# Head pairs of a delta-rule recurrence: one at a time in three interleaved generators, or two at a time in two

## The chip, the cores and the metric

The kernel runs on one core of one Trainium2 chip. The metric is device time in microseconds (us) for one execution of the whole program; before the change it is 2546.13 us, the median of three runs (2545.74 to 2553.71).

## What is computed

A decoder trunk of two residual layers, sequence 256, width 2048, all in fp32. The even layer (block attention and gated mixing) and the two gated MLPs are not touched. The odd layer is RWKV-7 time mixing with 32 heads of 64:

```python
def rwkv7_time_mix(h, mu, w_rkv, w_o, ...):
    r = xr @ w_rkv[0]; k = xk @ w_rkv[1]; v = xv @ w_rkv[2]
    w_log = -jax.nn.softplus(-(w0 + jnp.tanh(xw @ w1) @ w2)) - 0.5
    decay = jnp.exp(-jnp.exp(w_log))
    a = jax.nn.sigmoid(a0 + (xa @ a1) @ a2)
    g = jax.nn.sigmoid(xg @ g1) @ g2
    kk = k * k_k / max(norm of k * k_k per head, 1e-12)
    k = k * (1.0 + (a - 1.0) * k_a)
    def step(state, inp):                       # 256 steps in order
        sa = jnp.einsum('bhvk,bhk->bhv', state, -kk_t)
        state = state * w_t + sa[..., None] * (kk_t * a_t) + v_t[..., None] * k_t
        return state, jnp.einsum('bhvk,bhk->bhv', state, r_t)
    o = group norm of the outputs over each head, plus bonus sum(r * k * r_k) * v
    return (o * g) @ w_o
```

## The kernel before

**Dense products** are made exact by splitting fp32 operands into a high and a low part of type fp32r: ScalarE casts `w_hi` (L99, L115), VectorE subtracts `w_lo` (L101, L118). A K tile of a product with 256 positions is one matmul of 512 columns (`w_hi` by high and low input, L138 or L141) and one of 256 (L139).

**The odd layer's main loop** (`rwkv`, L679 to L685) goes over 16 pairs of heads, 128 channels each. The sequence is cut into 4 chunks of 64 positions, so that the recurrence becomes small matrix products in plain fp32. Three generators work on three pairs at a time, and `weave` merges their steps by weights: `pair_in(i)` makes k, r, the decays `E`, `Ei` and the norms `n4` and `bo` of pair i (32 dense K tiles); `pair_solve(i-1)` builds `bk` and the products `AQ`, and inverts the triangular matrices by 4 doubling levels of two products each (L840 into `Y`, L848 into `X`) and a last pair (L860, L868); `pair_out(i-2)` runs the 4 chunks one after the other (L904 and L906, ScalarE copy to `R`, L913, VectorE copy to `UV`, L918 and L932), then group norm and the gate product. A fp32 matmul stands as two records in the trace.

Two more iterations (i = 16, 17) drain the pipeline. Beside them `early` does the part of the output projection whose inputs are ready: `KO` = 12 of its 16 K tiles, for all 16 blocks of output. What is left (4 K tiles, `w_o1b`) is done after the loop by `residual`, two output blocks at a time: their sum is added into `x` (L191), and ScalarE, VectorE (L255) and GpSimd make the input of the next norm.

**Order.** The `weave` order is only a priority: a scheduler sets each engine's static order at build time, and engines then run in order, waiting by semaphores. `feed` casts the dense weights ahead of `dense_f` by `AHEAD` = 5 pieces. PSUM has 8 banks under 5 names (`BANKS`): `pd` dense, `pa` and `sc` two each, `po` and `pi` one each.

## Time and profile before

| | us |
|---|---|
| median of three runs | 2546.13 |
| the profiled execution | 2545.33 |
| its span on the core | 2543.5 |
| of it, from the first `pair_in` to the last `early` matmul (1223.6 to 1764.9) | 541.3 |
| of it, `residual` after that (1764.9 to 1797.5) | 32.6 |

PE is TensorE, PEld its weight loads, DVE VectorE, ACT ScalarE, POOL GpSimd. A PE that is busy need not be at its peak: ends of matmuls are modelled, and a small product keeps the engine from the next one longer than it streams. The distance from the start of one group of matmuls to the start of the next is therefore the better measure, and the timeline views give it.

### The profile page before, as it was taken

How to read it: one execution, taken by the hardware profiler on the slowest of the kernel's cores; microseconds unless marked ns; L12 is line 12 of the kernel's file. 1: busy time of each engine (PE TensorE's matmuls, PEld its weight loads, DVE VectorE, ACT ScalarE, POOL GpSimd, SP SyncE). 2: the span in 40 equal slices, each digit the busy share in tenths (PEclk: the TensorE clock that was granted, in tenths of full speed). 3: DMA queues.
4: the chain of work that ended last, by engine and by line, in shares of the span. 5: the costliest groups of instructions: out<-in, count | busy, mean ns of one | idle time of the engine just before them, and what ended most of it. 6: DMA issues, size and time to landing. Idle time of an engine off the chain costs nothing.

```text
span 2543.5 us, 49471 instructions
## 1 busy us (share of the span) xinstructions
PE 2497.4 (98%) x18884; PEld 2120.0 (83%) x18884; DVE 1871.7 (74%) x3813; ACT 1290.8 (51%) x2754; POOL 489.0 (19%) x810
## 2 busy tenths in 40 slices
PE   8999999999999999989999999999999999999998
PEld 6888888888888888878777777778888888888887
DVE  7768778888888645578777777877888888885444
ACT  6568655555555444454444444535555555554443
POOL 3100122222222100000233333321322222220000
PEclk9999999999999999999999999999999999999999
DMA  7554555555555666646322322235555555556664
GB/s 262 181 175 158 165 181 187 193 186 191 190 188 190 189 185 189 186 144 185 118 81 87 95 88 78 81 109 170 172 191 188 191 189 190 190 182 194 187 190 144
DMA packets 126493, 422.30 MB, mean 166 GB/s; under 512 B 14129, under 2 KB 20657, under 8 KB 126257
## 3 DMA queue, kind: packets, MB, share of 16 engines
q1 hardware_dynamic: 126112, 418.82, 52.6%
q8 instruction: 148, 2.42, 0.4%
q14 instruction: 89, 0.72, 0.1%
q10 hardware_dynamic: 144, 0.33, 0.0%
HBM read 417.00 MB, written 2.10 MB: 165 GB/s over the span
## 4 chain that ended last, share of the span: by engine, by line
PE 90%; DVE 5%; ACT 2%; POOL 1%; issue 1%; DMA 1%; SPq 0%; POOLq 0%; DVEq 0%; ACTq 0%
PE pd L170 20%; PE pd L171 11%; PE pi L170 10%; PE po L170 10%; PE pi L171 6%; PE po L171 6%; PE pd L138 5%; PE pd L139 3%; PE pd L173 1%; PE sc L614 1%; DVE w_lo L101 1%; PE po L906 1%; PE sc L913 1%; PE pd L215 1%; PE pd L214 1%
## 5 line engine op out<-in xcount | busy, mean ns | idle before, releaser
L101 DVE TENSOR_TENSOR w_lo<-w_raw,w_hi 128x512 fp32r<-128x512 f32 (+1 forms) x1392 | 1054.9, 788 | 317.4 <-ACT w_hi L99 292.2
L99 ACT CAST w_hi<-w_raw 128x512 fp32r<-128x512 f32 (+1 forms) x1392 | 792.3, 614 | 502.9 <-PE pd L170 139.8
L170 PE MATMUL pd<-xc,w_hi 128*128 128x512 f32 x1500 | 528.1, 392 | 1.6 <-DVE xc L255 1.0
L171 PE MATMUL pd<-xc,w_lo 128*128 128x256 f32 x1600 | 433.8, 281 | 0.0
L170 PEld LDWEIGHTS pd<-xc,w_hi 128*128 128x128 f32 x1500 | 281.4, 188 | 60.6 <-issue 2.7
L171 PEld LDWEIGHTS pd<-xc,w_lo 128*128 128x128 f32 x1600 | 301.9, 189 | 8.4
L170 PE MATMUL po<-xc,w_hi 128*128 128x512 f32 x750 | 264.8, 393 | 0.0
L170 PE MATMUL pi<-xc,w_hi 128*128 128x512 f32 x750 | 263.4, 392 | 0.0
L171 PE MATMUL po<-xc,w_lo 128*128 128x256 f32 x800 | 217.3, 282 | 1.9 <-DVE w_lo L101 1.9
L171 PE MATMUL pi<-xc,w_lo 128*128 128x256 f32 x800 | 216.9, 281 | 0.0
L170 PE MATMUL pd<-hc,w_hi 128*128 128x512 f32 x602 | 211.4, 393 | 0.0
L171 PE MATMUL pd<-hc,w_lo 128*128 128x256 f32 x616 | 169.7, 279 | 0.0
L170 PEld LDWEIGHTS po<-xc,w_hi 128*128 128x128 f32 x750 | 140.7, 188 | 29.5 <-issue 1.5
L170 PEld LDWEIGHTS pi<-xc,w_hi 128*128 128x128 f32 x750 | 140.7, 188 | 28.5
L138 PE MATMUL pd<-mx,w_hi 128*128 128x512 f32 x416 | 163.2, 418 | 0.0
L118 DVE TENSOR_TENSOR w_lo<-w_raw,w_hi 128x256 fp32r<-128x256 f32 x352 | 150.0, 461 | 16.7 <-ACT w_hi L115 15.6
L171 PEld LDWEIGHTS po<-xc,w_lo 128*128 128x128 f32 x800 | 150.9, 189 | 6.9 <-DVE w_lo L101 2.7
L243 POOL TENSOR_TENSOR sqacc<-sqacc,sq 128x256 f32<-128x256 f32 x70 | 61.8, 883 | 491.1 <-ACT sq L235 470.5
L171 PEld LDWEIGHTS pi<-xc,w_lo 128*128 128x128 f32 x800 | 150.9, 189 | 4.3
L115 ACT CAST w_hi<-w_raw 128x512 fp32r<-128x512 f32 x176 | 107.0, 620 | 79.2 <-PE pa L695 34.4
L170 PEld LDWEIGHTS pd<-hc,w_hi 128*128 128x128 f32 x602 | 112.8, 187 | 26.4
L139 PE MATMUL pd<-mx,w_lo 128*128 128x256 f32 x448 | 128.4, 298 | 0.0
(328 smaller groups left out, 4665.4 us busy)
## 6 DMA issues: line engine op xcount, KB each, us to landing
w_raw<-w_up SPq DMA_DIRECT2D x352, 512.0 KB, 4.1
w_raw<-w_dn SPq DMA_DIRECT2D x160, 512.0 KB, 3.7
w_raw<-w_kr SPq DMA_DIRECT2D x64, 512.0 KB, 4.3
w_raw<-w_eva SPq DMA_DIRECT2D x48, 512.0 KB, 4.2
w_raw<-w_out SPq DMA_DIRECT2D x32, 512.0 KB, 4.5
w_raw<-w_v SPq DMA_DIRECT2D x32, 512.0 KB, 3.8
w_raw<-w_evb SPq DMA_DIRECT2D x31, 512.0 KB, 4.4
w_raw<-w_dn SPq DMA_DIRECT2D x32, 256.0 KB, 2.7
```

Of the source, the lines that this page charges most:

```text
L99: nc.scalar.copy(hi[h], raw[h])
L101: nc.vector.tensor_sub(lo[h], raw[h], hi[h])
L115: nc.scalar.copy(hi[:, j:j + 512], raw[:, j:j + 512])
L118: nc.vector.tensor_sub(lo[:, j:j + pieces], raw[:, j:j + pieces], hi[:, j:j + pieces])
L138: nc.tensor.matmul(o, h, xc[k], start=k == 0, stop=False)
L139: nc.tensor.matmul(o[:, 0:S], l, xc[k][:, 0:S], start=False, stop=False)
L170: nc.tensor.matmul(o, h, xc[k], start=k == 0, stop=False)
L171: nc.tensor.matmul(o[:, 0:S], l, xh, start=False, stop=False)
L173: nc.tensor.matmul(o, h, xc[k], start=False, stop=True)
L214: nc.tensor.matmul(ps[t], xh, h, start=k == 0, stop=False)
L215: nc.tensor.matmul(ps[t], xh, l, start=False, stop=False)
L243: nc.gpsimd.tensor_add(self.nacc, self.nacc, sq)
```

## The change

`pair_solve` and `pair_out` become one generator `quad(j)`, which carries pairs 2j and 2j+1 through every step together: 34 steps, one after the other. The main loop has 9 iterations: `inputs(j)` makes two pairs while `quad(j-1)` runs. Each small product is issued for both pairs in one go, and the VectorE, ScalarE and GpSimd instructions behind it take both where the shapes allow. The sum of squares and the bonus are reduced in one instruction per pair, `nx` is spread by ScalarE instead of GpSimd, the gate weights of two pairs are cast together, and several tiles share a buffer (`bk` with `UV`, `nx` with `on`, `be` with `bv`). `KO` is 14: `early` takes 14 of 16 K tiles, `residual` 2. Its cut of the code, in its core:

```diff
-KO = 12
+KO = 14
@@ rwkv
-                for i in range(18):
-                    out = self.pair_out(i - 2, sp, w) if i >= 2 else iter(())
-                    solve = self.pair_solve(i - 1, sp, w) if 0 <= i - 1 < 16 else iter(())
-                    inp = self.pair_in(i, sp, w) if i < 16 else iter(())
...
-                    weave((out, 17), (solve, NA), (inp, NE[i - 16] if i >= 16 else NB))
+                def inputs(j):
+                    yield from self.pair_in(2 * j, sp, w)
+                    for i, _ in enumerate(self.pair_in(2 * j + 1, sp, w)):
+                        if j == 7 and i >= 12 and len(yc) < KO - 2:
+                            part(len(yc), min(len(yc) + 2, KO - 2))
+                        yield
...
+                for j in range(9):
+                    chain = self.quad(j - 1, sp, w) if j else iter(())
+                    lead(chain, 2)
+                    if j == 8:
+                        part(len(yc), KO)
+                    weave((chain, NC), (inputs(j), 2 * NB) if j < 8 else (early(0, KT), KT * 7))
@@ pair_in
-        nc.vector.tensor_reduce(bo, c4(pb[:, 0:S]), axis=AX.X, op=ALU.add)
+        for i, t in enumerate((sq, rk)):
+            for c in range(2):
+                nc.tensor.transpose(pb[:, i * S + c * P:i * S + (c + 1) * P], t[:, c * P:(c + 1) * P], self.ident)
+        nc.vector.tensor_reduce(n8.rearrange("p i n -> p (i n)"), pb.rearrange("p (n t) -> p n t", t=64),
+                                axis=AX.X, op=ALU.add)
@@ quad
+        for z, d in enumerate(ds):
+            nc.scalar.copy(nx[:, z], d["n4"].unsqueeze(2).to_broadcast([P, 4, 64]))
...
+        for z in Q:
+            pqs = [self.bank(n) for n in (("sc", "sc"), ("po", "pi"))[z]]
...
+        pts = [self.bank("sc") for _ in Q]
...
         for li, b in enumerate(LEVELS):
             py = self.bank("pi")
-            for i in range(4):
+            for i in range(8):
                 for q in range(4):
                     mm(py[qs[q], i * 16:(i + 1) * 16], AT(q, q % 2)[:, i], fh(X[qs[q], i]), start=True, stop=True)
...
-            pu = self.bank("pi")
-            for i in range(4):
+            pu = self.bank("po")
+            for i in range(8):
...
+            for z in Q:
+                for h in range(2):
+                    mm(pU[hu, z, h * 64:h * 64 + 64], Z[hu, 4 * z + 2 * h + g], R[hu, z, h * 64:h * 64 + 64],
+                       start=True, stop=True)
+            nc.vector.tensor_scalar_mul(UV[hu, :, c], pU[hu, :, 0:P], -1.0)
...
-        for i in range(4):
-            nc.scalar.activation(on[:, i], on[:, i], AF.Identity, scale=rs[:, i:i + 1], bias=mb[:, i:i + 1])
+        for i in range(8):
+            nc.scalar.activation(on8[:, i], on8[:, i], AF.Identity, scale=rs[:, i:i + 1], bias=mb[:, i:i + 1])
...
-NA, NB = 13.5, 20.5
-ME, NE = 8, (30, 40)
+NB, NC = 20.5, 34
```

The order of the built programs shows it at three places of a full round of the loop. In its names `pi`, `po`, `sc`, `pa`, `pd` are PSUM banks, `tl` the inputs of the decay product, `m1` and other masks lie in `csr`. Lines shift: L840 and L848 become L855 and L863, L765 and L769 become L769 and L775, L906 to L932 become L917 to L949, L118 becomes L124.

TensorE, in the levels, where the transposes of `rkt` (bonus of the next pair) fall between them. Before:

```order
L848 MATMUL pi<-Y,Z 32x16 x16
L138 MATMUL pd<-mx,w_hi 128x512
L139 MATMUL pd<-mx,w_lo 128x256
L138 MATMUL pd<-mx,w_hi 128x512
L960 MATMUL sc<-ident,on 128x128 x2
L139 MATMUL pd<-mx,w_lo 128x256
L769 MATMUL pa<-ident,rkt 128x128 x2
L860 MATMUL pi<-X,AQ 32x32 x8
```

Now:

```order
L863 MATMUL po<-Y,Z 32x16 x32
L147 MATMUL pd<-xc,w_hi 128x512
L775 MATMUL pa<-ident,ksq 128x128 x2
L855 MATMUL pi<-X,AQ 32x16 x32
L705 MATMUL pa<-tl_11368,w_hi 128x256
L706 MATMUL pa<-tl_11368,w_hi 128x256
L707 MATMUL pa<-tl_11368,w_lo 128x256
L705 MATMUL pa<-tl_11369,w_hi 128x256
L706 MATMUL pa<-tl_11369,w_hi 128x256
L707 MATMUL pa<-tl_11369,w_lo 128x256
L863 MATMUL po<-Y,Z 32x16 x32
L775 MATMUL pa<-ident,rkt 128x128 x2
```

A level's product has 32 matmuls instead of 16, and two levels now follow closely around the transposes.

TensorE, in the chunks of the recurrence, where the state `st` enters. Before:

```order
L918 MATMUL sc<-UV,tm 64x64 x2
L932 MATMUL po<-UV,AQ 64x64 x2
L809 MATMUL pa<-ar,bk 128x128 x4
L904 MATMUL po<-st,ar 128x128
L906 MATMUL po<-UV,AQ 64x64 x2
L809 MATMUL pa<-ar,bk 128x128 x4
L913 MATMUL sc<-R,Z_19074 64x64 x2
L139 MATMUL pd<-mx,w_lo 128x256
```

Now:

```order
L931 MATMUL sc<-UV,tm 64x64 x4
L949 MATMUL po<-UV,AQ 64x64 x2
L949 MATMUL pi<-UV,AQ 64x64 x2
L145 MATMUL pd<-mx,w_lo 128x256
L147 MATMUL pd<-mx,w_hi 128x512
L144 MATMUL pd<-xc,w_hi 128x512
L913 MATMUL po<-st,ar 128x128
L913 MATMUL pi<-st,ar 128x128
L917 MATMUL po<-UV,AQ 64x64 x2
L917 MATMUL pi<-UV,AQ 64x64 x2
L145 MATMUL pd<-xc,w_lo 128x256
```

The products of two pairs, into banks `po` and `pi`, stand together.

VectorE, between the products `AQ` and the first level's input `X`. Before:

```order
L118 TENSOR_TENSOR w_lo<-w_raw,w_hi 128x256 x5
L814 TENSOR_TENSOR AQ<-pa,csr 128x512 x2
L914 TENSOR_SCALAR UV<-sc 64x128
L830 TENSOR_TENSOR Z<-AQ,csr 32x128 x2
L921 SCALAR_TENSOR_TENSOR sr<-sr,fs,sc 128x64
L832 TENSOR_TENSOR Z<-Z,csr 128x128
L927 SCALAR_TENSOR_TENSOR st<-sr,fs,csr 128x128
L833 STREAM_TRANSPOSE X<-Z 128x128
```

Now:

```order
L830 TENSOR_TENSOR AQ<-sc,csr 128x512 x2
L124 TENSOR_TENSOR w_lo<-w_raw,w_hi 128x256 x2
L830 TENSOR_TENSOR AQ<-po,csr 128x512
L830 TENSOR_TENSOR AQ<-pi,csr 128x512
L124 TENSOR_TENSOR w_lo<-w_raw,w_hi 128x256
L838 TENSOR_TENSOR Z<-AQ,csr 32x256 x2
L124 TENSOR_TENSOR w_lo<-w_raw,w_hi 128x256
L847 TENSOR_TENSOR Z<-Z,csr 128x256
L124 TENSOR_TENSOR w_lo<-w_raw,w_hi 128x256
L848 STREAM_TRANSPOSE X<-Z 128x256
```

Four `AQ` instead of two and the masks of both pairs come before one `X`, with five pieces of `w_lo` between them.

## Rows read from the trace of the kernel before

**Rows 1.** The page: the span.

```profile
span 2543.5 us, 49471 instructions
```

**Rows 2.** Busy time by stretch (start:end, length, engines' busy us, clock, DMA): loop, residual.

```profile
1223.60:1764.90 541.30, 527.22 (x7698) 408.63 (x7697) 419.96 (x1296) 243.81 (x614) 176.09 (x336) 1.00 0.31 97
...
1764.90:1797.50 32.60, 29.53 (x228) 27.87 (x226) 32.10 (x55) 22.86 (x52) 14.69 (x17) 1.00 0.50 163
```

**Rows 3.** Timeline of TensorE (start us, length us), one level's product within dense tiles.

```profile
1400.18 0.28 PE L139 MATMUL pd<-xc,w_lo 128*128 128x256 f32 x1
1400.39 0.44 PE L848 MATMUL pi<-Y,Z 32*32 32x16 f32 x32
1400.76 0.50 PE L138 MATMUL pd<-xc,w_hi 128*128 128x512 f32 x1
1401.10 0.28 PE L139 MATMUL pd<-xc,w_lo 128*128 128x256 f32 x1
...
1401.44 0.28 PE L139 MATMUL pd<-xc,w_lo 128*128 128x256 f32 x1
```

**Rows 4.** Timeline of TensorE, products of the chunks and of `AQ`.

```profile
1410.74 0.44 PE L913 MATMUL sc<-R,Z 64*64 64x64 f32 x4
1411.11 0.51 PE L138 MATMUL pd<-mx,w_hi 128*128 128x512 f32 x1
...
1412.24 0.34 PE L918 MATMUL sc<-UV,tm 128*64 128x64 f32 x4
1412.41 0.40 PE L932 MATMUL po<-UV,AQ 128*64 128x64 f32 x4
1412.73 0.71 PE L809 MATMUL pa<-ar,bk 64*128 64x128 f32 x8
```

**Rows 5.** Groups by line, 1550 to 1950 us (xcount, busy us, mean ns).

```profile
L948 ACT ACTIVATE on<-on,mb,rs 128x64 f32<-128x64 f32 x26 | 9.4, 429 | 14.2 <-POOL mb L946 13.3 <-DVE X L850 0.9
L848 PE MATMUL pi<-Y,Z 32*32 32x16 f32 x672 | 9.2, 180 | 0.0
```

**Rows 6.** Timeline of TensorE from the end of an r product to `rkt`.

```profile
1402.59 0.40 PE L141 MATMUL pd<-xc,w_hi 128*128 128x512 f32 x1
...
1405.97 0.44 PE L769 MATMUL pa<-ident,rkt 128*128 128x128 f32 x2 [0.48 <-DVE rkt L765]
```

**Rows 7.** Timeline of VectorE over the same time.

```profile
1404.20 0.96 DVE L763 TENSOR_TENSOR ar<-kr,E 128x256 f32<-128x256 f32 x1
1405.09 0.83 DVE L765 SCALAR_TENSOR_TENSOR rkt<-kr,vec,kp 128x256 f32<-128x256 f32 x1
```

**Rows 8.** Waits of TensorE, 1223.6 to 1764.9 us (us in total, times, longest).

```profile
PE pa L769 <- DVE rkt L765: 6.3, 13, 0.5
PE pa L819 <- DVE AQ L814: 1.1, 1, 1.1
PE sc L960 <- POOL on L951: 0.9, 1, 0.9
```

**Rows 9.** Timeline of VectorE, from `AQ` to `X`.

```profile
1414.13 1.42 DVE L118 TENSOR_TENSOR w_lo<-w_raw,w_hi 128x256 fp32r<-128x256 f32 x4
1415.47 1.27 DVE L814 TENSOR_TENSOR AQ<-pa,csr 128x512 f32<-128x512 f32 x2
...
1416.97 1.04 DVE L830 TENSOR_TENSOR Z<-AQ,csr 32x128 f32<-32x128 f32 x2
...
1418.70 0.30 DVE L833 STREAM_TRANSPOSE X<-Z 128x128 f32<-128x128 f32 x1
```

**Rows 10.** Timeline of VectorE in `residual`, one round of two output blocks.

```profile
1781.34 1.35 DVE L255 SCALAR_TENSOR_TENSOR xc<-x,vec,xc 128x256 fp32r<-128x256 f32 x2
...
1783.28 1.83 DVE L101 TENSOR_TENSOR w_lo<-w_raw,w_hi 128x512 fp32r<-128x512 f32 x2
1785.03 0.96 DVE L255 SCALAR_TENSOR_TENSOR xc<-x,vec,xc 128x256 fp32r<-128x256 f32 x1
```

## The prediction

> **What bounds the kernel now.** I read the page first, then busy time by stretch, then TensorE's timeline. In the loop over head pairs, 541.3 us of a span of 2543.5 [rows 1, 2], TensorE is busy 527, VectorE 420 and ScalarE 244. The other stages are not touched, but for `residual` behind the loop. So TensorE sets the end here, and the question is what fills it. The timeline tells: a dense K tile (L138 with L139) takes 0.34 us, 1401.10 to 1401.44 [rows 3]. Around one product of a level, two L139 that would stand 0.34 apart stand 0.92 apart (1400.18 to 1401.10). One small group costs 0.58 us. Of this the group holds the engine for 0.37 (1400.39 to 1400.76); the other 0.21 is the break in the dense stream, a later entry and a first dense matmul that takes 0.34 instead of 0.23. L913 has 4 records instead of 32 and holds the engine for the same 0.37 [rows 4]. So a good part of each small group doesn't depend on how much is in it. That is what carrying two pairs together saves.

> **Fewer groups and breaks.** I counted, in the order of both programs, small groups (neighbouring products of one line) and runs of them between dense matmuls, from the first `pair_in` to the last `early` matmul: 560 groups in 320 runs before, 320 groups in 240 runs now. (Runs fall by less than half: with three generators many groups of different ones already stood side by side, as L918, L932, L809 do [rows 4].) The same records stream in all. What one group start costs beside its records has to be bounded. In a level 32 records start within 0.44 less the 0.18 of the last, 0.26 us [rows 3, 5], which leaves 0.11 of its 0.37. L918 holds 0.17 for four records, L932 0.32 [rows 4]; by the first L913 would leave 0.20 of its 0.37, and the first itself leaves hardly 0.05. I take 0.13, near the level, which has the most groups. 240 × 0.13 = 31 us (12 to 48). 80 breaks × 0.21 = 17 us. Together 48 us less (29 to 65).

> [...]

> **`KO` of 14.** `early` does 2 more K tiles for 16 blocks: 32 × 0.34 = 11 us more in the loop's last round, where TensorE has no other idle time to put it in. `residual` loses the same products, but isn't bound by them: a round of two output blocks lasts 3.69 us (1781.34 to 1785.03), and VectorE is busy all through it [rows 2, 10]. Of the round the two `w_lo` pieces hold 1.75 (1783.28 to 1785.03); one of them goes, 0.88 us. Over 7 full rounds that is 6 us less (0 if GpSimd's or ScalarE's part is next, 9 at most, if the piece that goes is the slow one). This part by itself costs 5 us.

> **New waits.** Before, `pair_out` and `pair_solve` ran beside each other, so that each had a whole round per pair. Now `quad` is one chain of 34 steps, each waiting for the step before, in a round of two pairs. What stands between two steps is dense work, 2 to 10 half tiles by the order, fixed at build time. I went through a full round with the durations of the rows, and found five places where TensorE arrives early:

> - *First level.* From the first `AQ` to the end of `X` VectorE needed 3.53 us (1415.47 to 1419.00 [rows 9]). Now there are two more `AQ` (0.6 each), larger masks and transpose (0.5 in all), five pieces of `w_lo` (0.34 each, from four in 1.42) instead of three instructions of `pair_out` (with the rest 0.9, what `AQ`, masks and `X` leave of the 3.53): some 6.0 us. TensorE has the second pair's `AQ` (0.8), six transposes (0.7), 19 dense half tiles of 0.17 and a break to do, 5 us. Wait 1.0.
> - *Bank `sc`.* The transposes of `bk` now use the two banks that the first `AQ` read. Wait 0.25; when the old solve stood alone, L819 waited 1.1 us once for `AQ` [rows 8].
> - *`rkt`.* L769 came 3.38 us after the last r product (1402.59 to 1405.97), behind `ar` 0.96 and `rkt` 0.83 on VectorE, and waited 0.48, 6.3 us in 13 waits [rows 6 to 8]. These instructions are the same now and stand twice in a round, once with `Y` ahead of them. 0.2 more per round. The transposes of `rkt` now stand ahead of the next level, and what is queued behind them on TensorE waits too.
> - *Group norm.* ScalarE now does 8 of L948 in one go, not 4; 4 × 0.43 = 1.7 us later at most [rows 5] for the transposes of `on`, whose longest old wait was 0.9 [rows 8]. Meanwhile TensorE has more dense work ahead of them. Wait 0.8 more. Casts of `w_hi` stand behind them on ScalarE, but `feed` is 5 pieces ahead.
> - *The rest.* VectorE's four instructions for the decays stand ahead of the last level's `X` (0.35), and each of the chunk steps has 0 to 0.1 too little (0.3).

> 2.9 us per round. 7 rounds have `quad` beside `inputs`: 20 us. In the last, 12 or 16 dense half tiles stand between the steps, and nothing waits. The bounds are 0 (scheduler's slack is enough, as nearly everywhere in the trace of before) and 40 (every place twice as late).

> **Edits at nothing.** VectorE's instructions for two pairs cost less than two for one pair each, but VectorE is not the bound; nor is GpSimd, from which `nx` moves to ScalarE (244 of 541 us busy, two copies more per round). The joint gate cast, one `gng` load instead of two and the joint reduction are hidden by dense work. If TensorE had no more of it, each would cost its duration once a round, below 1 us. The drain's order (`part` in pieces) moves casts of finished pairs ahead of `early`, on engines with room.

> **Sum.** −48 + 11 − 6 + 20 = −23 us against the profiled execution's 2545.3: 2522.3. The median of the runs stands 0.8 above that execution: 2523.

> **The rivals.**
> - *The waits don't show.* Then −43: 2503. For it: outside `rkt` TensorE's waits of before came once each [rows 8], in an order that the same scheduler made. Against: rounds of two pairs, one chain. Chance 0.22.
> - *The waits eat the gain.* About 40 us of them, −3: 2543. For it: VectorE is busy for 420 of 541 us, and every step of the chain that ends on it may stand behind a piece of `w_lo`. Chance 0.16.
> - *The chain becomes the bound.* The place is rounds 1 to 7; the dense work between steps no longer covers a step's way through TensorE, VectorE or ScalarE and back, and TensorE waits at most of the 34. The gain of 43 is gone when a round loses 43/7 = 6.1 us, 0.18 per step. At 0.3 per step it is 10.2 × 7 = 71 us, +28: 2574. For it: doubled products stream longer (0.26 more in a level) before the next engine may start. Against: fixed distances that I added up, mostly just enough. Chance 0.11.
> - *A doubled group starts its further records closer together.* [...] The rows speak against it. Chance 0.03.

> **How the numbers follow.** The forecast, 2512 to 2538, has 0.48. A measurement here can tell about 0.3%, 7.6 us, from no change. Faster by more: 0.48 + 0.22 + 0.03 = 0.73. Within: 0.16. Slower: 0.11. The range reaches from 2500, no new waits, to 2546, 43 us of them; it leaves out the third rival and the ends of the others.

> **What would show it.** The loop stage should shrink from 541 to about 524 us, and `residual` from 33 to 27. A group of 64 records should hold TensorE for about 0.63 us, and its break should still cost 0.21; if it holds 0.74, nothing is saved by joining. TensorE's waits should stand at the first level (for `X`), at `rkt` and at the transposes of `on`. I am wrong if waits at the levels or chunks are long and many, if dense matmuls wait for `w_lo` or `w_hi`, or if `residual` keeps its 3.7 us a round.

## The result, and the profile after

| | before | after |
|---|---|---|
| median, us | 2547.38 (4 runs) | 2642.51 (4 runs, 2627.75 to 2654.51) |
| profiled execution / span | 2545.3 / 2543.5 | 2654.5 / 2652.7 |
| first `pair_in` to last `early` matmul | 541.3 | 656.1 |
| `residual` behind it, to `norm_end` | 32.6 | 25.6 |

The change makes the kernel slower, by a ratio of 1.0366 (95% interval 1.0309 to 1.0423). 2523 was forecast. All of the loss is in the loop. The profiled execution is the slowest of the four: it lost 109 us where the medians lost 95, and the sums below are for that execution.

The page of after: span, TensorE's busy tenths, its granted clock in tenths.

```profile
span 2652.7 us, 49018 instructions
...
PE   8999999999999999999899988899899999999998
...
PEclk9999999999999999999767787779999999999999
```

Busy time by stretch of after (start:end, length, engines, clock, DMA): loop, `residual`, and one round of two pairs, from its first `AQ` to the next round's. They answer to [rows 2].

```profile
1224.60:1880.70 656.10, 595.88 (x7763) 480.57 (x7762) 390.60 (x1112) 243.60 (x621) 153.67 (x240) 0.80 0.26 81
1880.70:1906.30 25.60, 19.62 (x131) 18.02 (x129) 25.46 (x48) 19.82 (x46) 12.55 (x17) 0.93 0.47 147
1409.80:1485.40 75.60, 68.10 (x917) 54.18 (x916) 42.07 (x124) 25.63 (x68) 19.23 (x32) 0.73 0.21 66
```

The same view for one stretch within that round, to which the text comes back below:

```profile
1419.90:1454.00 34.10, 34.10 (x603) 26.54 (x603) 15.00 (x46) 7.91 (x20) 2.73 (x6) 0.50 0.25 78
```

The same view of before, for one pair, with the clock held and with one short fall of it:

```profile
1383.50:1412.70 29.20, 28.54 (x460) 21.83 (x457) 23.02 (x73) 12.99 (x35) 10.94 (x21) 1.00 0.28 85
1500.30:1530.90 30.60, 29.94 (x458) 22.85 (x457) 22.91 (x73) 12.93 (x35) 10.95 (x21) 0.94 0.25 81
```

Two pairs took 58.4 us before, 57.1 of it TensorE's. The round of after takes 75.6, and the same products now fill 68.1. The clock column says why: 1.00 before, 0.73 in this round. In the traces of before and after the clock stood at 1.00 or at 0.50 (as from 1419.9 to 1454.0) and at no value between; in the seven rounds it stood at 0.5 for 256 us.

TensorE's waits in the loop of after (us in total, times, longest), for [rows 8]:

```profile
PE sc L986 <- POOL on L974: 24.2, 11, 3.4
PE pi L855 <- DVE X L848: 15.2, 8, 2.3
PE po L863 <- issue: 5.7, 4, 2.2
PE sc L845 <- DVE AQ L830: 5.0, 6, 1.2
...
PE pi L855 <- issue: 1.6, 3, 1.3
```

TensorE's timeline in after, at the transposes of `on` (L986) and around the first level (L855, L863; L144 and L145 are L138 and L139 of before):

```profile
1399.21 0.40 PE L144 MATMUL pd<-mx,w_hi 128*128 128x512 f32 x1
1402.98 0.69 PE L986 MATMUL sc<-ident,on 128*128 128x128 f32 x2 [3.38 <-POOL on L974]
...
1412.97 1.14 PE L845 MATMUL sc<-ident,bk 128*128 128x128 f32 x6 [1.16 <-DVE AQ L830]
...
1417.09 0.28 PE L145 MATMUL pd<-xc,w_lo 128*128 128x256 f32 x1
1419.12 0.72 PE L855 MATMUL pi<-X,AQ 32*32 32x16 f32 x64 [1.75 <-DVE X L848]
...
1420.27 0.41 PE L145 MATMUL pd<-xc,w_lo 128*128 128x256 f32 x1
1420.49 0.63 PE L144 MATMUL pd<-xc,w_hi 128*128 128x512 f32 x1
1420.91 0.41 PE L145 MATMUL pd<-xc,w_lo 128*128 128x256 f32 x1
...
1421.68 1.05 PE L863 MATMUL po<-Y,Z 32*32 32x16 f32 x64
```

After the wait of 1.75 us a dense K tile takes 0.64 (1420.27 to 1420.91), not 0.34, and a product of a level lasts 1.05, not 0.72. The clock fell at 1419.9 and came back at 1454.0, all through the levels, though TensorE had no idle time there. A shorter fall, 3.4 us, stands at the end of the wait of 3.38. That is the pattern of all seven rounds: 3 to 7 us at 0.5 behind L986, then 24 to 34 us behind L845 and L855, five times in one piece, twice as 3.4 us and, behind a gap for issue, 20 to 27 us more.

The last round, in which `early` runs beside `quad`, is different. It has the same wait ahead of the first level, but the clock stood at 0.5 for only 3.4 us (TensorE's timeline at that wait, and the stretch at 0.5):

```profile
1787.34 0.71 PE L855 MATMUL pi<-X,AQ 32*32 32x16 f32 x64 [1.82 <-DVE X L848]
...
1788.50:1791.90 3.40, 3.40 (x73) 2.73 (x72) 2.28 (x7) 0.00 (x0) 0.00 (x0) 0.50 0.72 218
```

There 5 to 16 dense half tiles stand between the products of the levels; in the seven rounds it is 1 to 6. So the length of the wait does not by itself set how long the clock stays down.

**Where the 115 us came from.** The seven rounds last 519.8 us in all, against 7 × 58.4 = 409 before. TensorE idles for 53.7 us in them (9 before): 44 more. A round of two pairs at full clock keeps TensorE busy for 53.05 us (measured below, in the last experiment), against 57.1: 28 less. What is left, 519.8 − 53.7 − 7 × 53.05 = 95 us, is the clock. 44 − 28 + 95 = 111; the other 4 lie in the ends of the loop, where `early` grew. The 95 is an estimate, because the 53.05 comes from another order of the same products.

### The profile page after: what moved, and what is told of

It reads as the page before. It is cut to its first block, busy times and chain, and to the rows that moved or that the text cites. A ratio compares the mean times of both kernels' runs of the same rounds, so it can differ in the third digit from the quotient of the medians.

```text
span 2652.7 us, 49018 instructions
## 1 busy us (share of the span) xinstructions
PE 2557.3 (96%) x18852; PEld 2183.0 (82%) x18852; DVE 1836.7 (69%) x3621; ACT 1288.3 (49%) x2754; POOL 464.7 (18%) x714
## 3 DMA queue, kind: packets, MB, share of 16 engines
q8 instruction: 148, 2.42, 0.4%
## 4 chain that ended last, share of the span: by engine, by line
PE 89%; DVE 5%; POOL 3%; ACT 2%; issue 1%; DMA 0%; SPq 0%; DVEq 0%; POOLq 0%; ACTq 0%
PE pd L176 19%; PE pd L177 10%; PE pi L176 10%; PE po L176 10%; PE pd L144 6%; PE pi L177 5%; PE po L177 5%; PE pd L145 4%; PE po L863 1%; PE pd L179 1%; PE pi L855 1%; PE sc L620 1%; PE pd L221 1%; DVE w_lo L124 1%; PE pd L222 1%
## 5 line engine op out<-in xcount | busy, mean ns | idle before, releaser
L144 PE MATMUL pd<-mx,w_hi 128*128 128x512 f32 x448 | 204.4, 479 | 0.0
L124 DVE TENSOR_TENSOR w_lo<-w_raw,w_hi 128x256 fp32r<-128x256 f32 x368 | 153.2, 455 | 26.6 <-ACT w_hi L121 24.8
L145 PE MATMUL pd<-mx,w_lo 128*128 128x256 f32 x480 | 160.1, 343 | 0.0
L192 ACT COPY half<-pd 128x256 f32<-128x256 f32 x132 | 49.2, 373 | 210.7 <-PE pd L179 119.6
```

The costliest lines, as they stand in the source:

```text
L124: nc.vector.tensor_sub(lo[:, j:j + pieces], raw[:, j:j + pieces], hi[:, j:j + pieces])
L144: nc.tensor.matmul(o, h, xc[k], start=k == 0, stop=False)
L145: nc.tensor.matmul(o[:, 0:S], l, xc[k][:, 0:S], start=False, stop=False)
L192: self.nc.scalar.copy(t, o[:, S:2 * S])
```

## Experiments

**1. Is the clock lost by waits, whatever the mix of work?** The kernel before, with a longer way to the transposes of `on`:

```diff
         nc.gpsimd.tensor_add(on, on, bv)
+        for _ in range(5):
+            nc.gpsimd.tensor_scalar_mul(on, on, 1.0)
```

> The kernel before, with one edit: five more GpSimd instructions on `on` (each multiplies by 1, some 0.7 us) ahead of the transposes of `on`, once per pair, so that TensorE has to wait there as it does in after. Theory A: the waits of 2 to 3.5 us come in most of 16 rounds (some 45 us), and behind each the granted clock falls to 0.5 for 3 to 30 us although the mix of work is that of before; time 2610 to 2750. Theory B: the waits alone, 30 to 55 us, with the clock at 1.00; time 2575 to 2600.

Measured 2686.72 us in its one execution (before 2548.41). The waits of this kernel and the stretch of one pair:

```profile
PE sc L962 <- POOL on L953: 78.9, 16, 5.7
...
1388.50:1425.90 37.40, 32.04 (x459) 24.58 (x457) 22.75 (x73) 12.97 (x35) 15.11 (x26) 0.86 0.21 67
```

The waits were longer than planned: 14 of the 16 lasted 5.3 to 5.7 us. This pair grew by 8.2 us: 4.7 more idle time, and 3.5 more busy time for the same products, at a clock of 0.86. The clock fell at each of those 14 waits, for 10 to 20 us. Of the other two, with `early` beside them, one of 2.2 us went without a fall and one of 2.3 us was followed by 3.4 us at 0.5. From the first `AQ` to the last, idle time grew by 65 us and busy time by 69. So a wait can cost more than its length, in the old order of work too; with waits as short as those of after it was not tried there.

**2. Fill the waits.** A first try put products of 128x256, which nobody reads, ahead of the transposes of `on` and of the first level, in the bank that the waiting product itself uses; the transposes of `bk` went to bank `pa`.

```diff
+            for _ in range(24 if z == 0 else 0):
+                mm(pg[:, S:2 * S], wh[:, 0:P], w["sg"][0][:, 0:S], start=True, stop=True)
...
-        pts = [self.bank("sc") for _ in Q]
+        pts = [self.bank("pa") for _ in Q]
```

> After, with products put where TensorE would stand idle, whose results are overwritten before anyone reads them: 24 of 128x256 (0.115 us each at the full level) ahead of the first pair's transposes of `on`, 14 ahead of the first level; the transposes of `bk` go to bank `pa`, so that they no longer wait for `AQ`. No wait of the chain gets shorter by this. Theory A (the clock): in after the granted clock stood at 0.5 for 262 us of the loop, each time behind a wait of TensorE of 1.2 to 3.4 us; half of that, 131 us, is lost to it. With the gaps filled the clock stays at 1.00, the loop falls from 656 us to 525 to 545, and the time to 2520 to 2545. Theory B (the waits themselves and the doubled groups in a serial chain): the gaps are filled but not shortened, so the loop stays at 640 to 665 us and the time at 2625 to 2665.

> Only the 24 products ahead of the transposes of `on` (L986 of after). Theory A: the short falls of the clock behind that wait go (some 42 us at 0.5 in all), the long ones behind `AQ` and `X` stay (some 220 us); time 2610 to 2635. If the longest wait is the one that starts the long falls too, it comes to 2520 to 2560. Theory B: no change, 2630 to 2665.

> Only the 14 products ahead of the first level, and the transposes of `bk` in bank `pa`. Theory A: the long falls go, the short ones behind the transposes of `on` stay with their 7 waits of 3.4 us; time 2535 to 2570. Theory B: the wait for `AQ` goes (5 us in 4 times), the rest stays, 2625 to 2655.

Measured 2671.78 us (ratio to before 1.0499, 1.0463 to 1.0534), 2671.24 and 2653.54. The first two are slower than after, the third lies within after's own spread (2627.75 to 2654.51), but they don't speak for theory B: the filling products waited themselves, for the bank (waits of the first kernel; L988 and L854 are those products):

```profile
PE sc L988 <- ACT g L986: 16.8, 7, 3.1
PE pi L854 <- DVE AQ L830: 15.1, 7, 2.2
```

So hardly anything was filled. The second try uses a bank of its own, and edges that fix the order put each block behind the dense matmul that stood last ahead of the wait.

```diff
+    def fill(self, i, n, x):
+        d = self.bank("pa")
+        for _ in range(n):
+            m = self.nc.tensor.matmul(d[:, 0:S], x[:, 0:P], x[:, 0:S], start=True, stop=True)
+            self.dums.append((m, i))
```

> After, with work put into TensorE's three waits of a round, rounds 1 to 7: products of 128x256 from `xk` into a bank `pa` that nobody reads, 30 between the last dense matmul ahead of the first transposes of `on` and those (3.45 us at 0.115 each, for a wait of 3.4), 10 ahead of the transposes of `bk` (1.15 for 1.2), 16 ahead of the first level (1.84 for 1.8). The order of TensorE fixes them at these places, and all else stands as in after. The chain's steps take as long as before; TensorE only doesn't stand idle. Theory A (the clock is lost behind these waits, and that loss is most of it): clock at 1.00 but for single falls, loop 656 to 530 to 560, time 2520 to 2555. Theory B (the chain's latency is what costs; the clock is a by-product): the filled waits still end when the data come, loop 640 to 660, time 2630 to 2660.

> As the run with all three waits filled, but only the 30 products ahead of the transposes of `on`. Theory A, if each wait brings its own fall: the falls behind the transposes of `on` go, the long ones behind `AQ` and `X` stay, 2600 to 2635; if the longest wait sets off all of it: 2520 to 2560. Theory B: 2630 to 2660.

> Only the 10 products ahead of the transposes of `bk` and the 16 ahead of the first level. Theory A: the long falls of 20 to 34 us go, the short ones of 3 to 7 us behind the transposes of `on` stay; 2540 to 2580. Theory B: 2630 to 2660.

Measured 2641.23 us (1.0370, 1.0344 to 1.0395), 2649.1 and 2645.82: no gain. Theory A's numbers were wrong. Most of the waits were filled (at L986 27.8 us in all became 7.5, at the first level 15.2 became 3.4, ahead of the transposes of `bk` 5.0 became 0.6), and the falls behind L986 went in six of seven rounds. In the seven rounds TensorE's idle time fell from 53.7 to 34.2 us and the time at 0.5 from 256 to 154, but the filling is 45 us of work (7 × 56 × 0.115), so that the total hardly moved. A fall of 14 to 24 us still came in each round, in six of them beside a gap of another kind (in the first behind a wait of 0.89 us for `Y`). TensorE's timeline of the run with all three filled (L709 the filling, L880 and L890 the levels):

```profile
1411.46 2.07 PE L709 MATMUL pa<-mx 128*128 128x256 f32 x16
1413.72 0.72 PE L880 MATMUL pi<-X,AQ 32*32 32x16 f32 x64 [0.19 <-DVE X L871]
...
1415.23 0.72 PE L890 MATMUL po<-Y,Z 32*32 32x16 f32 x64
...
1416.55 0.73 PE L880 MATMUL pi<-X,AQ 32*32 32x16 f32 x64
1421.13 0.80 PE L145 MATMUL pd<-xc,w_hi 128*128 128x512 f32 x1 [3.85 <-issue]
```

Behind the third product of the levels at full clock TensorE stood for 3.85 us, which the timeline puts down to issue; no engine is named. A piece of 16 KB started in the queue `q8`, of the kind `instruction`, at 1418.8, and the next matmul came 2.3 us later. (The page of after counts 148 such pieces, 2.42 MB, and 37704 matmuls and weight loads, some 255 to a piece. That the pieces hold TensorE's instructions is my guess from these counts; no view shows it.) It is so for all six gaps of over 1 us in this run's levels and all five in after's: 2.2 to 2.6 us from the start of a piece to the end of the gap. A doubled product of a level is 64 matmul records and 64 weight loads in 0.7 us. In the loop of before, where half as many stand together, waits for issue are 0.3 us in all; in after, where most levels ran at a clock of 0.5, they are 7.3, and in this run 18.1.

**3. Thin out the levels.** The last kernel with four dense products of 128x512 (`NW`) ahead of each of the other seven level products:

```diff
+            m = self.wide(t, NW, w["xk"][0]) if j in FILL else None
             pu = self.bank("po")
```

> The run with all three waits filled, and four dense products of 128x512 (0.23 us each) more ahead of each of the other seven products of the levels, rounds 1 to 7: 7 x 7 x 0.92 = 45 us of work that nobody reads. In that run the clock still fell in each round, each time behind a gap of 2.1 to 3.9 us within the first levels for which no other engine is named; TensorE's next instruction came there 2.2 to 2.5 us after a 16 KB piece of the instruction queue had started (1418.8 to 1421.1). Theory C (a doubled level takes 128 instructions in 0.7 us, the supply of instructions runs dry, the gap brings the clock down, and the sparse levels keep it down): with more columns and fewer instructions per us the gaps and the falls go, and adding 45 us of work makes the loop shorter, 590 to 625 us against that run's 645, time 2575 to 2610. Theory B (the chain's latency): the work adds to the chain, loop 675 to 700, time 2665 to 2695.

Measured 2644.66 us (1.0374, 1.0352 to 1.0396), between the two expectations. 45 us of work were added and the time grew by 3. The rounds say more. Stretches from first `AQ` to first `AQ`, the same work in each:

```profile
1336.40:1416.40 80.00, 77.56 (x1006) 63.08 (x1006) 41.84 (x120) 25.60 (x68) 20.74 (x31) 0.83 0.20 62
1484.00:1550.90 66.90, 65.33 (x1000) 53.77 (x1000) 42.39 (x120) 25.62 (x68) 19.73 (x31) 1.00 0.24 74
1550.90:1617.20 66.30, 64.96 (x1000) 53.58 (x1000) 42.32 (x120) 25.54 (x68) 19.66 (x30) 1.00 0.23 76
```

In three of seven rounds the clock never fell, and they took 66.3 to 67.6 us, 66.9 in the mean. Two with a fall of 27.3 us took 80.0 and 81.3. So a fall of 27.3 us goes with 13 to 14 us more, 12 to 12.5 of them in TensorE's busy time. In one of the three rounds without a fall TensorE waited 1.41 us for issue all the same. The rounds hold 12.9 us of filling (56 × 0.115 and 28 × 0.23); without it TensorE's work in the two undisturbed ones shown is 52.1 to 52.4 us, less than the 57.1 of before. The change's saving is there, and it is seen where the clock holds.

Those two rounds lost 12 to 12.5 us of busy time in 27.3 us at 0.5, which is 0.44 to 0.46 of it; the loop of after lost less, some 95 in 256, 0.37, though only 9.4 of the 256 were idle. A dense K tile lost 0.30 of its 0.64 us there, a product of a level only 0.33 of its 1.05.

**4. Cut the chain elsewhere.** The end of `quad` (group norm, gate, transposes of `on`) becomes a generator `tail` that runs in the next round beside the next `quad`. Tags are regrouped to make room, `KO` is 12, `bk` is transposed into `pa`.

```diff
+                    tail = self.tail(j - 2, sp, w) if j > 1 else iter(())
...
-                    weave((chain, NC), (inputs(j), 2 * NB) if j < 8 else (early(0, KT), KT * 7))
+                    weave((chain, NC if j < 8 else NC + 9), (tail, NT), (inputs(j), 2 * NB) if j < 8 else (early(0, KT), KT * 7))
```

> Two generators again, cut elsewhere than before: the end of `quad` (group norm, gate product, transposes of `on`) becomes one of its own and runs in the next round beside the next `quad`, so that the wait for the group norm has other work to stand in (by the order 14.8 us of TensorE's work lie between the last product into `on` and its transposes, 4.5 in after). `KO` is 12, and the transposes of `bk` use bank `pa`. Theory C: the waits at the transposes of `on` go, the falls at the first level and in the levels stay; 2590 to 2625. Theory B: the chain per round is 9 us shorter, so most of the loss goes; 2540 to 2580.

Measured 2605.56 us in one execution, as theory C had it. The wait at the transposes of `on` is gone (0.9 us in all); the first level waits for `X` 41.9 us in 8 times. Now the dense half tiles are spread by edges, some 5 ahead of each level product (`PLAN[e]` is the half tile of the round behind which product e of the chain stands):

```diff
+PLAN = (14, 14, 22, 26, 50, 55, 60, 65, 70, 75, 80, 85, 90, 94, 99, 107, 114, 121)
+    def pin(self, t, j, e):
+        if j < 7:
+            self.dums.append((t, 128 * (j + 1) + PLAN[e] - 1))
```

> As the run with the end of `quad` as its own generator, and the dense half tiles are spread by hand: TensorE's order puts some 5 of them (0.87 us) ahead of each product of the levels, 24 between the transposes of `bk` and the first level, 5 to 10 ahead of each step of the chunks. No work is added. Theory C: no gaps in the levels, the clock stays at 1.00, and the gain of fewer groups shows: 2490 to 2540. Theory B: the sum of the chain's latencies is the bound in either order, 2560 to 2620.

Measured 2567.17 us (1.0074, 1.0053 to 1.0095), above C's range and in B's. The waits for issue in the levels are small (5.6 us in all), but the gate's product now waited for its weights:

```profile
PE sc L722 <- DVE w_lo L107: 25.8, 6, 4.3
PE sc L720 <- ACT w_hi L105: 7.3, 6, 1.2
```

So the gate's weights are loaded ahead of the group norm:

```diff
+        wh2, wl2 = self.load_w([a["w_l2"][2 * j + z, :, 2 * P:4 * P] for z in Q], 2 * P)
         on8 = on.rearrange("p z i n -> p (z i) n")
```

> The run with the end of `quad` as its own generator and the dense half tiles spread by hand, with two edits: the gate's weights are loaded and cast at the start of that generator (in that run their DMA was issued 3 us before TensorE stood at the gate product, which waited 1.2 us for `w_hi` and 4.3 for `w_lo` in six rounds, 33 us in all), and three half tiles more stand ahead of the first level. Theory C (gaps cost their length and then half of the clock's low time): the 33 us go, and with them the falls behind them, some 45 of 60 us at 0.5, worth 20 more; rounds of 62 us become 54 to 56, the time 2505 to 2530, faster than before. Theory B (the chain's latency sums up to a round in any order): the wait moves to the next step of the chain, 2550 to 2570.

Measured 2566.29 us (1.0069, 1.0044 to 1.0094), as B had it: the wait moved. VectorE's timeline, GpSimd's, and TensorE's wait in this kernel:

```profile
1452.93 0.43 DVE L867 TENSOR_TENSOR Z<-Z,csr 128x256 f32<-128x256 f32 x1 [4.88 <-POOL Z L858]
1453.28 0.95 DVE L125 TENSOR_TENSOR w_lo<-w_raw,w_hi 128x256 fp32r<-128x256 f32 x1
...
1449.43 0.68 POOL L829 TENSOR_TENSOR be<-ta,Ei 128x256 f32<-128x256 f32 x1
1450.06 1.27 POOL L919 COPY UV<-vt 64x512 f32<-64x512 f32 x2
1451.41 1.49 POOL L858 TENSOR_TENSOR Z<-AQ,csr 32x256 f32<-32x256 f32 x2
...
PE pd L146 <- DVE w_lo L125: 30.0, 9, 4.5
```

GpSimd's two masks of `Z` stood behind the group norm, `be` and `UV`; VectorE stood 4.88 us for them, and the dense stream for the `w_lo` behind that. So these masks move to VectorE:

```diff
-            (nc.vector if q % 2 else nc.gpsimd).tensor_mul(
+            nc.vector.tensor_mul(
```

> The run with the gate's weights loaded early, and one edit: all four masks of `Z` on VectorE (two of them stood on GpSimd). In that run VectorE stood 4.88 us at the sum of `Z` in each round, because GpSimd's masks were queued behind the group norm's four products and sums, `be` and `UV`; the pieces of `w_lo` queued behind that on VectorE, and TensorE's dense stream waited 4.5 us for them, 30 us in all. Theory C: these waits go, and with them most of the falls of the clock; 2515 to 2540, faster than before. Theory B (something else of the chain is next each time): 2550 to 2570.

Measured 2538.66 us (6 runs; before 2551.75 in 9), ratio 0.995 (0.9934 to 0.9967), in theory C's range: 4% faster than after, and faster than before by 0.5%, which is small but clear of the noise. Two of its rounds, without a fall:

```profile
1316.20:1373.60 57.40, 52.98 (x914) 42.75 (x915) 42.86 (x123) 25.59 (x68) 17.59 (x29) 1.00 0.28 87
1555.10:1612.00 56.90, 53.13 (x915) 42.83 (x915) 43.11 (x123) 25.67 (x68) 17.66 (x29) 1.00 0.28 88
```

53.05 us of work against 57.1, at full clock, and 4 us idle. Five other rounds still spend 7 to 10 us at 0.5.

## Why the prediction was wrong

The step that failed is the sum itself: a term was missing. Every duration was taken at full clock, and I never asked what a wait does to it. In its place the clock stood at 0.5 for 256 us of the loop, and that term is some 95 us. The next step in fault is the new waits.

- *Fewer groups and breaks* (−48; 29 to 65). Right in kind and within its bounds, but sized too high. TensorE's work fell by 4.05 us per round of two pairs, over eight quads some 32 us. The group of 64 holds the engine 0.65 us where the clock holds (experiment 2, 1413.72 to 1414.37), 0.63 was expected, and the dense matmul behind it is the longer one (0.34 us, 1414.37 to 1414.71), as in the break of [rows 3].
- *`KO` of 14.* `residual` lost 7.0 us, 6 were forecast. The 11 in the loop can't be told apart from the rest.
- *New waits* (+20; 0 to 40). They came to 44, just above the upper bound, most of them at places named, but with other sizes. First level: 1.8 in a usual round, for 1.0. Bank `sc`: 0.9 to 1.2 in four of seven rounds, for 0.25. Group norm: 3.4, for 0.8. `rkt`: none, for 0.2 more than the old wait; `ar` and `rkt` take 0.42 and 0.48 now, not 0.96 and 0.83 [rows 7]. Waits for issue, some 1 us a round, weren't in the list.
- *Group norm* was the worst of them. I counted only ScalarE's four more instructions. The chain in after runs through GpSimd:

```profile
1396.35 0.17 DVE L959 BATCH_NORM_AGGREGATE mv<-s 128x2 f32<-128x6 f32 x1
1396.61 0.33 POOL L273 TENSOR_SCALAR rs_tmp<-mv 128x8 f32<-128x8 f32 x1
1397.23 1.85 POOL L274 TENSOR_TENSOR rs<-rs_tmp,mhalf 128x8 f32<-128x8 f32 x1
1399.16 0.49 POOL L966 TENSOR_TENSOR mb<-mb,rs 128x8 f32<-128x8 f32 x1
1399.69 2.76 ACT L968 ACTIVATE on<-on,mb,rs 128x64 f32<-128x64 f32 x8 [2.36 <-POOL mb L966]
1401.20 0.72 POOL L973 TENSOR_TENSOR on<-on,gng 128x256 f32<-128x256 f32 x1 [1.54 <-ACT on L968]
1402.20 0.72 POOL L974 TENSOR_TENSOR on<-on,bv 128x256 f32<-128x256 f32 x1
```

  The inverse root waits for all eight columns (the last aggregate stood 0.8 us behind other work) and takes 1.85 us for eight, 1.05 for four before. From the last product of the chunks to the transposes it is 8.6 us (1394.38 to 1402.98), and TensorE's work between them is 5.2.
- *The rivals.* The third had the right sign: the chain became the bound. Its place was not "most of the 34 steps" but three of them, and its price, 6.3 us more idle time a round, is just above the 6.1 from which it decides. By that alone the time would have been about 2560 (2546 + 44 − 28, 4 more at the ends of the loop, 7 less in `residual`). The rest is the clock, which no case of mine held. That dense work could simply be placed elsewhere was assumed too easily: experiment 4 needed the chain cut, the order fixed, the gate's weights loaded early and the masks moved before the gain showed. Theory B was right about two of the four steps there, theory C about the first and the last. No run shows a figure behind the 0.03 for the last rival: the group of 64 held the engine 0.65 us, no less than the 0.63 expected.

What stays open: whether the doubled levels bring the clock down without any gap. In no round did they stand close together without one of 0.9 us or more ahead of them or among them. But the one fall in the loop of before (3.4 us, from 1524.9) came in a pair whose idle time, 0.66 us, was that of its neighbours, so a longer gap isn't needed for every fall. And that the waits for issue come from the supply of instructions is argued from their times alone and not shown; no run changed the queue, and thinning the levels brought them from 18.1 to 11.6 us.

## What to carry to other kernels

Cost a wait on TensorE twice: its length, and a share of the time for which the clock stays at 0.5 behind it, 0.34 to 0.46 in these runs. That time is not set by the wait alone: behind waits of 1.8 to 2.3 us ahead of the first level of after it was 31 to 34 us five times and 3.4 us three times. Before two chains that cover each other are made one, add up the one's whole way through all engines, GpSimd's queue first, against the dense work left to cover it. Two pairs in one group saved TensorE 4.05 us a round here, but what is saved is only worth something where the next step's data are there already.
